# The MLP's matmuls of a hybrid decoder layer walk their 256 columns in interleaved chunks

## The chip, the cores and the metric

The program runs on 1 core of one Trainium2 chip. The metric is the device time of one execution in microseconds (us). Everything is computed in float32; the large products use the float32r type for both operands.

## What is computed

One decoder layer over 256 tokens with 16 learned meta tokens ahead of them and a width of 2048. Three token mixers (HGRN2, Mamba-2, RWKV-7) share a normed input and one combined projection, are gated, merged and projected. Only the channel mixer behind them is touched by the change:

```python
u = rmsnorm(h, ln2_w[l])
h = h + valid * (jnp.square(jax.nn.relu(u @ w_mlp_in[l])) @ w_mlp_out[l])
...
return rmsnorm(h, lnf_w)[:, CHUNK:]
```

`w_mlp_in` is 2048 x 8192 and `w_mlp_out` 8192 x 2048.

## The kernel before

Activations are held transposed: channels on the 128 partitions, tokens along the free dimension. A tile `[128, 16, 256]` is 2048 channels of 256 tokens. Each float32 operand is split into a high and a low part of type float32r, and a product is the sum of three: high by high, low by high weights, high by low weights.

`weights` (L213) fetches a weight piece of 128 x 1024 floats through SyncE's queue (L222, tile `raw`), copies it on ScalarE to the high part `wh` (L201) and takes the difference on VectorE for the low part `wl` (L202). Three buffers stand for each of `wh` and `wl`; weights are fetched and split ahead of the products that use them.

`product` (L229) makes one output tile of 128 channels by 256 tokens in a PSUM buffer `pt` (three of them in turn). For the MLP it issues 16 x 3 = 48 matmuls (L237, L238, L239). Each loads a 128 x 128 piece of weights into TensorE and streams 256 columns, the tokens, of one slice of the activations past it; all 48 accumulate on the same 256 places of PSUM.

The MLP (L1179 to L1204) runs over four quarters of the hidden width, `qd` 0 to 3. Each quarter has two stages of 16 products, so 768 matmuls to a stage, and there are eight stages in this order, called stage 1 to 8 below:

- stages 1, 3, 5, 7 (`mi`): the activations `zh`, `zl` by `w_mlp_in`; ScalarE takes the ReLU out of PSUM (L1185), VectorE squares (L1187), and the result is split into `hh`, `hl`.
- stages 2, 4, 6, 8 (`mo`): `hh`, `hl` by `w_mlp_out`; in stage 2 ScalarE copies the sum to `macc` (L1192), in stages 4 and 6 VectorE adds it there (L1194), and in stage 8 VectorE multiplies it by the norm's factor `r2` (L1200) and adds it to the residual `h1` (L1201).

The last norm follows: squares are summed over channels by a matmul with ones (L1206, L1209), and 12 tiles on VectorE and 4 on GpSimd are scaled (L1214) and stored (L1216).

Instructions are put in order by a scheduler at build time. On TensorE the products of the MLP follow each other in program order, stage after stage.

Of the kernel before, what the change touches and what calls it, by code (L numbers as in the profile page):

```python
# [20 lines left out]
KT = D // P  # L21
# [129 lines left out]
def tile_hybrid(ctx: ExitStack, tc: tile.TileContext, a, out, dbg=None):  # L151
    nc = tc.nc
    dbg = dbg or {}
    mult, add, sub = ALU.mult, ALU.add, ALU.subtract
    act, vec, pe = nc.scalar, nc.vector, nc.tensor

    def pool(stack, name, side=None, space=None, bufs=1):
        kw = {"side": side} if side else {}
        if space:
            kw["space"] = space  # L160
        return stack.enter_context(tc.tile_pool(name=name, bufs=bufs, reuse_waits="tile", **kw))
# [13 lines left out]
    def V(k, j=0, n=1, rows=slice(0, P)):  # L175
        return vecs[rows, VCOL[k] + j:VCOL[k] + j + n]
# [13 lines left out]
    def uname(s):  # L190
        cnt[0] += 1
        return f"{s}_{cnt[0]}"

    def trunk_psum(w):
        return ps_t.tile([P, 512], F32, tag="t", bufs=3, name=uname("pt"))[:, :w]
# [4 lines left out]
    def split(dst_h, dst_l, src):  # L200
        act.copy(dst_h, src)  # L201
        vec.tensor_tensor(dst_l, src, dst_h.bitcast(F32), sub)  # L202
# [10 lines left out]
    def weights(key, ahead=True):  # L213

        first, n = PIECE[key]
        parts = []
        for k in range(n):
            with tc.high_priority() if ahead else ExitStack():
                n_raw[0] += 1
                rpool, bufs = more_raw[n_raw[0] % len(more_raw)]  # L220
                raw = rpool.tile([P, 8, P], F32, tag="raw", bufs=bufs, name=uname("raw"))
                nc.sync.dma_start(raw, a["w"][first + k])  # L222
                wh = wp.tile([P, 8, P], F32R, tag="wh", bufs=3, name=uname("wh"))
                wl = wp.tile([P, 8, P], F32R, tag="wl", bufs=3, name=uname("wl"))
                split(wh, wl, raw)
            parts.append((wh, wl))
        return parts

    def product(key, hi, lo, tok, kts=KT, ahead=True):  # L229

        n = tok.stop - tok.start
        ps = trunk_psum(n)
        last = kts // 8 - 1
        for k, (wh, wl) in enumerate(weights(key, ahead)):
            for j in range(8):
                kt = 8 * k + j
                pe.matmul(ps, lhsT=wh[:, j], rhs=hi[:, kt, tok], start=(kt == 0), stop=False)  # L237
                pe.matmul(ps, lhsT=wh[:, j], rhs=lo[:, kt, tok], start=False, stop=False)  # L238
                pe.matmul(ps, lhsT=wl[:, j], rhs=hi[:, kt, tok], start=False,  # L239
                          stop=(k == last and j == 7))  # L240
        return ps

# [56 lines left out]
    def proj(key, tok=ALL, ahead=True):  # L299
        ps = product(key, uh, ul, tok, ahead=ahead)  # L300
        vec.tensor_tensor(ps, ps, rstd1[:, tok], mult)
        return ps
# [40 lines left out]
    for k in range(2):  # L343
        t = r1.tile([P, T + 1], F32, name=f"prev{k}")
# [19 lines left out]
    ps = proj("wl", ahead=False)  # L364
# [3 lines left out]
    ps = proj("aldt", ahead=False)  # L368
    shifted(ps, 25, alr[0:112], slice(0, 112))
    for j in range(2):  # L370
        ps = proj(("gl", j), REAL2)
# [155 lines left out]
    r2 = {}  # L527
# [552 lines left out]
    RT = slice(0, NR)  # L1080

    def branch_parts(o):
        hi = gp.tile([P, 8, NR], F32R, tag="oh", bufs=2, name=uname("oh"))
        lo = gp.tile([P, 8, NR], F32R, tag="ol", bufs=2, name=uname("ol"))
        for k in range(4):
            s = slice(2 * k, 2 * k + 2)
            split(hi[:, s], lo[:, s], o[:, s])
        return hi, lo
# [6 lines left out]
    def up_first(c, hi, lo):  # L1095
        g = gate_back("gr", c)
        ps = product(("upr", c), hi, lo, RT, 8)
        vec.tensor_tensor(mixed[:, c], ps, g, mult)

    def up_next(n, c, hi, lo, g):  # L1100
        ps = product((n, c), hi, lo, RT, 8)
        t = gp.tile([P, NR], F32, tag="bt", bufs=2, name=uname("bt"))
        vec.tensor_tensor(t, ps, g, mult)
        vec.tensor_tensor(mixed[:, c], mixed[:, c], t, add)
# [8 lines left out]
    hi, lo = branch_parts(o_r)  # L1113
# [4 lines left out]
    hi, lo = branch_parts(o_m)  # L1118
# [10 lines left out]
    hi, lo = branch_parts(o_h)  # L1129
# [14 lines left out]
    zh = ep.tile([P, 16, NR], F32R, name="zh")  # L1144
    zl = ep.tile([P, 16, NR], F32R, name="zl")
    acc2 = ep.tile([P, NR], F32, name="acc2")
    r2 = ep.tile([P, NR], F32, name="r2")
    macc = ep.tile([P, 16, NR], F32, name="macc")

    def et(tag, bufs=2):  # L1150
        return ep.tile([P, NR], F32, tag=tag, bufs=bufs, name=uname(tag))

    def add_square(c, src):
        s = et("sqe")
        act.activation(s, src, AF.Square)
        if c == 0:
            vec.tensor_copy(acc2, s)
        else:
            vec.tensor_tensor(acc2, acc2, s, add)

    for c in range(16):
        xr = et("xr", 3)
        nc.scalar.dma_start(xr, a["xt"][:, c, NM:])
        ps = product(("out", c), mh, ml, RT)
# [9 lines left out]

    act.activation(r2, pn, AF.Ln, bias=eps_n, scale=1.0 / D)
    act.activation(r2, r2, AF.Exp, scale=-1.0)
    st_y = ExitStack()
    yp = pool(st_y, "yp", side="right")
    for qd in range(4):  # L1179
        hh = yp.tile([P, 16, NR], F32R, tag="hh", bufs=2, name=uname("hh"))  # L1180
        hl = yp.tile([P, 16, NR], F32R, tag="hl", bufs=2, name=uname("hl"))
        for c in range(16):
            ps = product(("mi", 16 * qd + c), zh, zl, RT)
            r = et("rl")
            act.activation(r, ps, AF.Relu)  # L1185
            s = et("rs")
            vec.tensor_tensor(s, r, r, mult)  # L1187
            split(hh[:, c], hl[:, c], s)
        for c in range(16):
            ps = product(("mo", qd, c), hh, hl, RT)  # L1190
            if qd == 0:
                act.copy(macc[:, c], ps)  # L1192
            elif qd < 3:
                vec.tensor_tensor(macc[:, c], ps, macc[:, c], add)  # L1194
            if qd == 2:
                vec.tensor_tensor(macc[:, c], macc[:, c], r2, mult)
                vec.tensor_tensor(h1[:, c], h1[:, c], macc[:, c], add)
            if qd == 3:
                t = et("rs")
                vec.tensor_tensor(t, ps, r2, mult)  # L1200
                vec.tensor_tensor(h1[:, c], h1[:, c], t, add)  # L1201
                if c < 15:
                    add_square(c, h1[:, c])
                    act.activation(h1[:, c], h1[:, c], AF.Copy, scale=V("lnf", c))  # L1204
# [110 lines left out]
```

## Time and profile before

| What | us |
|---|---|
| median of 2 runs | 1935.1 (1934.91 to 1935.28) |
| the profiled execution's own time | 1936.93 |
| its span, first to last instruction | 1935.1 |
| TensorE busy with matmuls in it | 1906.0 (98%) |
| the eight MLP stages in it, one after the other | 733.6 (from 1187.18 to 1920.77) |

The span is what the profile's views cover; the execution's own time is 1.8 us more. PE is TensorE's matmuls, PEld its weight loads, DVE VectorE, ACT ScalarE, POOL GpSimd, SPq SyncE's queue. A matmul's duration in a row runs from its start to its modelled end and overlaps with those of the next ones; how fast TensorE works is told by how many matmuls it starts in a stretch.

### The profile page before, as it was taken

To read this page: it belongs to the slowest core of one execution; us is meant where nothing else is said; L and a number is where in the kernel's file an instruction comes from. 1 tells how busy PE (TensorE), PEld (TensorE's weight loads), DVE (VectorE), ACT (ScalarE), POOL (GpSimd) and SP (SyncE) were. 2 spreads that over 40 slices of the span, in tenths; PEclk is the share of its full clock that TensorE was granted. 3 is DMA by queue.
4 is the path that set the end of the run, shared out by engine and by line. 5 is a ranking of instruction groups with operands and counts; after the bars stand their busy time and mean duration, and the time that the engine had idled before them with its cause. 6 is when DMAs were issued, how large, how long until landed. Compare 5 with 4: busy or idle time off the path is not lost.

```text
span 1935.1 us, 39773 instructions
## 1 busy us (share of the span) xinstructions
PE 1906.0 (98%) x16220; PEld 1866.0 (96%) x16220; DVE 1242.9 (64%) x1992; ACT 1048.3 (54%) x1857; POOL 185.5 (10%) x318
## 2 busy tenths in 40 slices
PE   6999999999999999999999999999999999999997
PEld 6999999999999999999999999999999999999997
DVE  7878676567956566777677765544455555665565
ACT  5666666566556667766564455444444344334453
POOL 4020111111111111112111000000000000000000
PEclk9999999999999999999999999999999999999999
DMA  5556544445554445445656776555555555555552
GB/s 211 183 179 202 164 150 135 146 154 158 175 174 147 145 144 193 144 150 168 200 168 213 247 218 190 182 184 185 185 186 185 186 183 181 185 185 183 185 185 99
DMA packets 104119, 340.39 MB, mean 176 GB/s; under 512 B 18216, under 2 KB 21432, under 8 KB 103936
## 3 DMA queue, kind: packets, MB, share of 16 engines
q1 hardware_dynamic: 91904, 315.25, 51.0%
q0 software_dynamic: 8576, 17.67, 3.0%
q10 hardware_dynamic: 3456, 4.93, 0.7%
q8 instruction: 127, 2.08, 0.5%
q14 instruction: 56, 0.46, 0.1%
HBM read 327.72 MB, written 10.08 MB: 175 GB/s over the span
## 4 chain that ended last, share of the span: by engine, by line
PE 97%; DVE 1%; DMA 0%; issue 0%; ACT 0%; SPq 0%; DVEq 0%; POOLq 0%
PE pt L239 29%; PE pt L237 29%; PE pt L238 29%; PE px L1025 1%; PE px L551 1%; PE px L657 0%; PE px L639 0%; PE px L694 0%; PE px L565 0%; PE px L559 0%; DVE macc L1214 0%; PE px L480 0%; PE px L623 0%; PE px L627 0%; PE px L661 0%; PE px L848 0%
## 5 line engine op out<-in xcount | busy, mean ns | idle before, releaser
L202 DVE TENSOR_TENSOR wl<-raw,wh 128x1024 fp32r<-128x1024 f32 x592 | 725.6, 1226 | 452.1 <-ACT wh L201 444.8
L201 ACT CAST wh<-raw 128x1024 fp32r<-128x1024 f32 x592 | 620.4, 1049 | 706.2 <-PE pt L238 491.1
L237 PE MATMUL pt<-uh,wh 128*128 128x256 f32 (+3 forms) x2048 | 587.6, 287 | 9.2 <-ACT wh L201 9.2
L239 PE MATMUL pt<-uh,wl 128*128 128x256 f32 (+3 forms) x2048 | 587.9, 287 | 4.0 <-DVE wl L202 4.0
L238 PE MATMUL pt<-ul,wh 128*128 128x256 f32 (+3 forms) x2048 | 587.6, 287 | 1.7 <-DVE ul L285 1.7
L237 PEld LDWEIGHTS pt<-uh,wh 128*128 128x128 f32 x2048 | 387.8, 189 | 12.6 <-ACT wh L201 9.2
L239 PEld LDWEIGHTS pt<-uh,wl 128*128 128x128 f32 x2048 | 387.7, 189 | 8.1 <-DVE wl L202 4.6
L238 PEld LDWEIGHTS pt<-ul,wh 128*128 128x128 f32 x2048 | 387.2, 189 | 6.3 <-DVE ul L285 2.6
L239 PE MATMUL pt<-zh,wl 128*128 128x256 f32 x1024 | 290.0, 283 | 0.0
L238 PE MATMUL pt<-zl,wh 128*128 128x256 f32 x1024 | 289.8, 283 | 0.0
L237 PE MATMUL pt<-zh,wh 128*128 128x256 f32 x1024 | 289.8, 283 | 0.0
L239 PE MATMUL pt<-hh,wl 128*128 128x256 f32 x1024 | 288.0, 281 | 0.0
L238 PE MATMUL pt<-hl,wh 128*128 128x256 f32 x1024 | 288.0, 281 | 0.0
L237 PE MATMUL pt<-hh,wh 128*128 128x256 f32 x1024 | 287.8, 281 | 0.0
L237 PEld LDWEIGHTS pt<-zh,wh 128*128 128x128 f32 x1024 | 196.6, 192 | 0.0
L239 PEld LDWEIGHTS pt<-zh,wl 128*128 128x128 f32 x1024 | 196.6, 192 | 0.0
L238 PEld LDWEIGHTS pt<-zl,wh 128*128 128x128 f32 x1024 | 196.6, 192 | 0.0
L237 PEld LDWEIGHTS pt<-hh,wh 128*128 128x128 f32 x1024 | 192.8, 188 | 0.0
L238 PEld LDWEIGHTS pt<-hl,wh 128*128 128x128 f32 x1024 | 192.7, 188 | 0.0
L239 PEld LDWEIGHTS pt<-hh,wl 128*128 128x128 f32 x1024 | 192.7, 188 | 0.0
L239 PE MATMUL pt<-oh,wl 128*128 128x256 f32 x384 | 108.3, 282 | 0.0
L237 PE MATMUL pt<-oh,wh 128*128 128x256 f32 x384 | 108.2, 282 | 0.0
(451 smaller groups left out, 2388.0 us busy)
## 6 DMA issues: line engine op xcount, KB each, us to landing
raw<-in_w SPq DMA_DIRECT2D x592, 512.0 KB, 3.5
rcb<-sc_rc SPq DMA_DIRECT2D x8, 256.0 KB, 4.1
sc_gr<-gt POOLq DMA_DIRECT2D x16, 128.0 KB, 3.7
sc_gm<-gt POOLq DMA_DIRECT2D x16, 128.0 KB, 3.6
sc_gh<-gt POOLq DMA_DIRECT2D x16, 128.0 KB, 3.7
gin<-sc_gr POOLq DMA_DIRECT2D x16, 128.0 KB, 3.0
gin<-sc_gm POOLq DMA_DIRECT2D x16, 128.0 KB, 3.1
gin<-sc_gh POOLq DMA_DIRECT2D x16, 128.0 KB, 3.4
```

Source lines behind the costliest of these rows:

```text
L201: act.copy(dst_h, src)
L202: vec.tensor_tensor(dst_l, src, dst_h.bitcast(F32), sub)
L237: pe.matmul(ps, lhsT=wh[:, j], rhs=hi[:, kt, tok], start=(kt == 0), stop=False)
L238: pe.matmul(ps, lhsT=wh[:, j], rhs=lo[:, kt, tok], start=False, stop=False)
L239: pe.matmul(ps, lhsT=wl[:, j], rhs=hi[:, kt, tok], start=False, stop=(k == last and j == 7))
L551: pe.matmul(pk[e][:, c], lhsT=kt_[er, t], rhs=ar[er, :, t], start=True, stop=True)
L1025: pe.matmul(px[br, 2 * i + c], lhsT=xc, rhs=xc, start=True, stop=True)
```

## The change

`product` gets two views: `view` is laid over the moving operand (the 256 columns that are streamed) and, unless `view_out` is given, over the PSUM places that are written. `chunks(b, c)` cuts the 256 columns into `c` equal parts and takes `b` columns of the first part, `b` of the second and so on, then the next `b` of the first. Each column is still written to a place of its own and all 48 matmuls of a product use one order, so each sum has the same terms.

```diff
-    def product(key, hi, lo, tok, kts=KT, ahead=True):
+    def product(key, hi, lo, tok, kts=KT, ahead=True, view=lambda t: t, view_out=None):
...
+        po = (view_out or view)(ps)
...
-                pe.matmul(ps, lhsT=wh[:, j], rhs=hi[:, kt, tok], start=(kt == 0), stop=False)
+                pe.matmul(po, lhsT=wh[:, j], rhs=view(hi[:, kt, tok]), start=(kt == 0), stop=False)
...
+    def chunks(b, c=2):
+
+        return lambda t: t.rearrange("p (c a b) -> p a c b", c=c, b=b)
+
+    plain = lambda t: t
+
+    orders = [[chunks(16), chunks(16, 4)], [chunks(8), plain], [chunks(4), plain], [chunks(2), chunks(8)]]
...
-            ps = product(("mi", 16 * qd + c), zh, zl, RT)
+            ps = product(("mi", 16 * qd + c), zh, zl, RT, view=orders[qd][0])
...
-            ps = product(("mo", qd, c), hh, hl, RT)
+            if qd < 2:
+                ps = product(("mo", qd, c), hh, hl, RT, view=orders[qd][1])
+            elif qd == 2:
+
+                ps = product(("mo", qd, c), hh, hl, RT, view_out=chunks(8))
+                ps = chunks(8)(ps)
+            else:
+
+                ps = product(("mo", qd, c), hh, hl, RT, view=orders[qd][1], view_out=plain)
+                ps = ps.rearrange("p (a c b) -> p c a b", c=2, b=8)
             if qd == 0:
                 act.copy(macc[:, c], ps)
             elif qd < 3:
-                vec.tensor_tensor(macc[:, c], ps, macc[:, c], add)
+                m = macc[:, c] if qd == 1 else macc[:, c].rearrange("p (a c b) -> p a c b", c=2, b=8)
+                vec.tensor_tensor(m, ps, m, add)
...
                 t = et("rs")
-                vec.tensor_tensor(t, ps, r2, mult)
+                vec.tensor_tensor(t.rearrange("p (c a b) -> p c a b", c=2, b=8), ps,
+                                  r2.rearrange("p (c a b) -> p c a b", c=2, b=8), mult)
```

| Stage | columns read | places written |
|---|---|---|
| 1 | chunks of 16 from 2 halves | the same order |
| 2 | chunks of 16 from 4 quarters | the same order |
| 3 | chunks of 8 from 2 halves | the same order |
| 4 | in one run, as before | in one run, as before |
| 5 | chunks of 4 from 2 halves | the same order |
| 6 | in one run | chunks of 8; VectorE reads them back in runs of 8 |
| 7 | chunks of 2 from 2 halves | the same order |
| 8 | chunks of 8 from 2 halves | in one run; VectorE reads them back in runs of 8 |

No instruction changes its place on any engine. On TensorE, where stage 1 ends and stage 2 begins, this stands before (the shape at the end of a row is that of the places written; `pt` is the PSUM buffer, `zh`, `zl`, `hh`, `hl` the activations, `wh`, `wl` the weights):

```order
L237 MATMUL pt_16165<-zh,wh_16174 128x256
L238 MATMUL pt_16165<-zl,wh_16174 128x256
L239 MATMUL pt_16165<-zh,wl_16175 128x256
L237 MATMUL pt_16232<-hh_15158,wh_16235 128x256
L238 MATMUL pt_16232<-hl_15159,wh_16235 128x256
L239 MATMUL pt_16232<-hh_15158,wl_16236 128x256
```

At the same place on TensorE the changed kernel has:

```order
L239 MATMUL pt_16165<-zh,wh_16174 128x8x2x16
L240 MATMUL pt_16165<-zl,wh_16174 128x8x2x16
L241 MATMUL pt_16165<-zh,wl_16175 128x8x2x16
L239 MATMUL pt_16232<-hh_15158,wh_16235 128x4x4x16
L240 MATMUL pt_16232<-hl_15159,wh_16235 128x4x4x16
L241 MATMUL pt_16232<-hh_15158,wl_16236 128x4x4x16
```

The same buffers follow each other; only the shape differs: 8 x 2 chunks of 16, then 4 x 4 chunks of 16. The second place on TensorE is the end of stage 6 and the start of stage 7, before:

```order
L237 MATMUL pt_21324<-hh_19290,wh_21333 128x256
L238 MATMUL pt_21324<-hl_19291,wh_21333 128x256
L239 MATMUL pt_21324<-hh_19290,wl_21334 128x256
L237 MATMUL pt_21390<-zh,wh_21393 128x256
L238 MATMUL pt_21390<-zl,wh_21393 128x256
L239 MATMUL pt_21390<-zh,wl_21394 128x256
```

And in the changed kernel:

```order
L239 MATMUL pt_21324<-hh_19290,wh_21333 128x16x2x8
L240 MATMUL pt_21324<-hl_19291,wh_21333 128x16x2x8
L241 MATMUL pt_21324<-hh_19290,wl_21334 128x16x2x8
L239 MATMUL pt_21390<-zh,wh_21393 128x64x2x2
L240 MATMUL pt_21390<-zl,wh_21393 128x64x2x2
L241 MATMUL pt_21390<-zh,wl_21394 128x64x2x2
```

Again nothing moved: stage 6 writes 32 runs of 8 places, and stage 7 writes (and reads) 128 runs of 2. That stage 8 reads in runs of 8 is not seen in such rows, since it writes in one run.

## Rows read from the trace of the kernel before

**Rows 1.** The page: busy time of the engines, and the chain that ended last.

```profile
PE 1906.0 (98%) x16220; PEld 1866.0 (96%) x16220; DVE 1242.9 (64%) x1992; ACT 1048.3 (54%) x1857; POOL 185.5 (10%) x318
...
PE 97%; DVE 1%; DMA 0%; issue 0%; ACT 0%; SPq 0%; DVEq 0%; POOLq 0%
```

**Rows 2.** Windows of the eight MLP stages in turn, all instructions.

```profile
core 0: us, PE busy (x) PEld busy (x) DVE busy (x) ACT busy (x) POOL busy (x), PEclk, DMA share, GB/s
1187.18:1279.75 92.57, 92.57 (x772) 92.52 (x771) 50.38 (x65) 44.08 (x67) 0.00 (x0) 1.00 0.57 182
1279.75:1370.88 91.13, 91.13 (x770) 91.13 (x769) 39.87 (x34) 38.12 (x49) 0.00 (x0) 1.00 0.58 185
1370.88:1463.04 92.16, 92.16 (x770) 92.16 (x769) 49.28 (x62) 42.66 (x63) 0.00 (x0) 1.00 0.57 183
1463.04:1554.18 91.14, 91.14 (x770) 91.14 (x769) 46.07 (x49) 34.11 (x34) 0.00 (x0) 1.00 0.59 185
1554.18:1646.33 92.15, 92.15 (x770) 92.15 (x769) 49.72 (x63) 42.40 (x62) 0.00 (x0) 1.00 0.57 183
1646.33:1737.47 91.14, 91.14 (x770) 91.14 (x769) 57.48 (x79) 34.10 (x34) 0.00 (x0) 1.00 0.57 186
1737.47:1829.63 92.16, 92.16 (x770) 92.16 (x769) 50.48 (x65) 42.40 (x62) 0.00 (x0) 1.00 0.58 183
1829.63:1920.77 91.14, 91.14 (x770) 91.14 (x769) 54.90 (x77) 45.56 (x62) 0.00 (x0) 1.00 0.46 145
```

**Rows 3.** Waits in the MLP, longest first: who waited, total us, times, longest.

```profile
DVE wl L202 <- ACT wh L201: 292.1, 220, 3.9
ACT wh L201 <- PE pt L238: 203.7, 126, 1.8
...
DVE macc L1194 <- PE pt L239: 24.3, 30, 2.9
```

**Rows 4.** Single lines of TensorE: ns min/median/max, first and last start, form.

```profile
L495 PE MATMUL px<-ar,tkb x16: 191/248/270, 80.0 to 474.8; 128*96 128x32 f32 x16
L613 PE MATMUL px<-xtb,gt x128: 196/196/217, 225.7 to 683.4; 128*32 128x32 f32 x128
L551 PE MATMUL px<-ar,kt x64: 376/376/480, 213.7 to 628.8; 64*128 64x256 f32 x64
L1064 PE MATMUL px<-am,itm x16: 377/378/381, 806.4 to 1026.4; 96*128 96x256 f32 x16
```

**Rows 5.** Single lines of VectorE and ScalarE that read or write in short runs.

```profile
L1015 ACT ACTIVATE x<-sfx x64: 292/309/334, 722.0 to 1011.6; 128x128 f32<-128x128 f32 x64
L520 DVE COPY bigA<-bigB x2: 1052/1077/1102, 213.5 to 540.1; 68x1024 f32<-68x1024 f32 x2
```

**Rows 6.** Single lines that take the MLP's sums out of PSUM.

```profile
L1194 DVE TENSOR_TENSOR macc<-pt,macc x32: 418/425/426, 1471.6 to 1737.7; 128x256 f32<-128x256 f32 x32
L1200 DVE TENSOR_TENSOR rs<-pt,r x16: 418/424/426, 1838.1 to 1921.0; 128x256 f32<-128x256 f32 x16
```

**Rows 7.** Timeline of the end: start, us, what, and idle time before it.

```profile
1920.66 0.28 PE L239 MATMUL pt<-hh,wl 128*128 128x256 f32 x1
...
1920.98 0.42 DVE L1200 TENSOR_TENSOR rs<-pt,r 128x256 f32<-128x256 f32 x1 [3.90 <-PE pt L239]
1921.44 0.43 DVE L1201 TENSOR_TENSOR h<-h,rs 128x256 f32<-128x256 f32 x1
1921.90 0.42 ACT L1208 ACTIVATE sqe<-h 128x256 f32<-128x256 f32 x1 [4.74 <-DVE h L1201]
```

More of the change, by code (lines that the diff above doesn't have):

```diff
@@ L236, in product @@
                 kt = 8 * k + j
-                pe.matmul(ps, lhsT=wh[:, j], rhs=hi[:, kt, tok], start=(kt == 0), stop=False)
-                pe.matmul(ps, lhsT=wh[:, j], rhs=lo[:, kt, tok], start=False, stop=False)
-                pe.matmul(ps, lhsT=wl[:, j], rhs=hi[:, kt, tok], start=False,
+                pe.matmul(po, lhsT=wh[:, j], rhs=view(hi[:, kt, tok]), start=(kt == 0), stop=False)
+                pe.matmul(po, lhsT=wh[:, j], rhs=view(lo[:, kt, tok]), start=False, stop=False)
+                pe.matmul(po, lhsT=wl[:, j], rhs=view(hi[:, kt, tok]), start=False,
                           stop=(k == last and j == 7))
```

## The prediction

> **What bounds the kernel now.** I read the page first, then the windows of the MLP, then its waits, then single lines that resemble what the change makes. The page says that matmuls are in flight for 1906.0 of 1935.1 us and that 97% of the chain that ended last is TensorE [rows 1]. That alone proves little, since a matmul's row overlaps its neighbours, so the reader should look at counts: in each of the eight stages TensorE is busy without a gap, at a granted clock of 1.00, that is 2.4 GHz [rows 2]. A stage holds 768 matmuls by the code (the row counts one or two more, those that straddle the edges). Stages 3, 5 and 7 take 92.16 us, 120.0 ns a matmul; stages 2, 4, 6 and 8 take 91.14 us, 118.7 ns; stage 1, at 92.57 us, has a few tenths of start in it. 256 columns at one a cycle of 2.4 GHz would be 106.7 ns, so each matmul has 12 to 13 ns on top, and the columns cannot be going at half that pace.
>
> Who waits is told by the third view: in the MLP VectorE and ScalarE wait for one another and for TensorE (292.1 and 203.7 us), and no row has TensorE waiting for anybody [rows 3]. VectorE is busy 40 to 57 of some 91 us in a stage and ScalarE 34 to 46 [rows 2]. So one ns more or less per matmul is felt in full at the end, and work of other engines is not.
>
> **The change part by part.** No instruction is added, removed or moved, no transfer changes its place and no wait is added; what differs is the order of addresses within one instruction.
>
> Matmuls. 7 of 8 stages change, 7 x 768 = 5376 matmuls. In six stages (all but 4 and 6) the streamed columns come in runs, in six (all but 4 and 8) the PSUM places are written in runs: 16 runs a matmul in stages 1 and 2, 32 in stage 3, 64 in stage 5, 32 in stage 6 (writing only), 128 in stage 7, 32 in stage 8 (reading only). The columns stay 256. The question is whether a break between runs costs anything. The trace of before has no matmul with short runs on the writing side, and few on the reading side, so I bound it by the nearest rows.
>
> - Reading, TensorE: L495 streams 32 columns as two runs of 16, and its shortest row is 191 ns; L613 streams 32 columns in one run at 196 ns. L551 streams 256 columns as two runs of 128 at 376 ns, L1064 256 columns in one run at 377 to 378 ns [rows 4]. These lines differ in partitions too, and their ends are modelled, but neither pair shows a price for a break.
> - Many breaks, another engine: L1015 on ScalarE reads and writes 128 elements of which the first round of its loop has 128 runs of one and the last one run of 128. All 64 instructions lie between 292 and 334 ns [rows 5]. If the whole spread were due to runs, a break would cost 42 / 127 = 0.33 ns.
> - Supply of separate places: L520 on VectorE reads 1024 elements, each 128 bytes from the one before, in 1077 ns, 1.05 ns each [rows 5]. Stage 7 asks for a new place every second column, 0.83 ns at 2.4 GHz, a little faster than that row shows the memory to serve; stage 5 asks for one in 1.67 ns, and the others ask less often.
> - Below nothing: the trace has two paces for the same plain matmul, 120.0 and 118.7 ns, that go with the tile that is read. If the new order moved all 5376 to the quicker one, 5376 x 1.3 ns = 7 us would go.
>
> So the ends for the matmuls are -7 us and, at 0.33 ns for each of 16 + 16 + 32 + 64 + 32 + 128 + 32 = 320 runs in 768 matmuls, +81 us; doubling of stage 7 alone would be +92 us. I take 0, because the two rows that are TensorE's own show none, and they are nearest.
>
> The Trainium skill speaks against this choice: "PSUM — Partial Sum Buffer", section Specifications (TRN2), says that any access pattern that is not contiguous slows matmuls significantly. By that sentence the six stages that write in runs would suffer even at runs of 16, which no row here shows; it is the third rival below. The skill's "Advanced Engine Details and Errata", section Memory Cachelines, is milder: two consecutive elements should stand together in PSUM, and two hits on a line of SBUF are enough. By that sentence all eight orders are free, and its sum would be mine.
>
> Element-wise work. Stage 6's adds (L1194, 16 of the 32) and stage 8's products (L1200, 16) read PSUM in runs of 8. They take 425 and 424 ns [rows 6]. At worst I give each the double, 16 x 0.42 = 6.8 us to a stage; VectorE has over 33 us free in each of these stages and the three PSUM buffers give it two products, 11 us, to catch up, so this is hidden. Only the last L1200 stands on the path: it follows the last matmul and the sum of squares waits for it [rows 7]. Between 0 and 0.4 us; I take 0, by the same spread in rows of ScalarE.
>
> Sum. 1936.9 us for the profiled execution, plus 0. It is 1.8 us above the runs' median, so against the median this is 1935.1; with a few tenths for the tail and for the breaks I say 1935.5.
>
> **The rivals.**
> Stage 7 starves. With runs of two columns, TensorE wants a new place each 0.83 ns. If the memory gives one in 1.05 ns, as L520's row has it, 128 places take 134.6 ns in place of 106.7, a growth of 15 to 28 ns a matmul depending on whether the 12 to 13 ns on top remain: 768 x 15 to 28 = 11 to 21 us, 1946 to 1957. If a run of two costs as much as a run of four, the stage doubles: 1935 + 92 = 2027. For it: it is the only stage that asks for more than any row has shown. Against it: L520 may be at the pace of VectorE, not of the memory. It decides once a place takes longer than 0.83 ns.
>
> Every break costs a fixed bubble. At 0.33 ns, 81 us: 2016. For it: the spread of L1015. Against it: L551 and L495, which have a break and no price. It passes 2% (39 us, about what a measurement of this kernel tells from no change) from 39000 / (320 x 768) = 0.16 ns a break.
>
> Writing in runs costs TensorE the double, whatever the run's length. Stages 1, 2, 3, 5, 6 and 7 together are 551 us [rows 2], so 1935 + 551 = 2486. For it: no row of before has such a write, so nothing excludes it. Against it: nothing in the trace but analogy.
>
> Faster. To win 39 us, 5376 matmuls would have to lose 7.2 ns each of the 12 to 13 on top of their columns. The rows show 1.3 ns between tiles, nothing like it.
>
> **How the numbers follow.** No change within 10 us: 0.62. Stage 7 slower by 11 to 21 us: 0.10, within 2% too. Stage 7 doubled: 0.08. A bubble for each break above 0.16 ns: 0.09. Writes doubled: 0.08. Faster by over 2%: 0.03. So within 2% is 0.72, slower 0.25, faster 0.03. The likeliest case's own range is 1928 to 1945: 7 us for the quicker pace below, 10 above. To leave out no more than 2 in 10 the range goes up to the doubled stage 7 and the bubble: 1928 to 2030; what is left out is the doubled writes, the gain and the worst of the bubbles.
>
> **What would show it.** In the windows of the changed kernel each stage should take 91.1 to 92.6 us, with 768 matmuls and the same idle rows. Stage 4 is plain and must stay at 91.1 in any case; if it moves, the cause is not the order. Stage 7 alone long means supply; growth by 16, 16, 32, 64, 32, 128, 32 means a price per break; stages 1, 2, 3, 5, 6, 7 long alike, with 8 as before, means writes; stage 8 long with 6 as before means reads. TensorE appearing among those who wait in the MLP would show that I misjudged the cover on VectorE.

## The result and the profile after

The changed kernel takes 1988.1 us (two runs, 1988.06 to 1988.18) against 1935.1 before. The ratio is 1.0274, 95% interval 1.0249 to 1.0298: slower, by 53 us. That is inside the range, but well above the time that I gave as likeliest (1935.5); how my cases stand to it is told further below.

The page of the profile after, the same two lines as in [rows 1]:

```profile
PE 1958.9 (99%) x16220; PEld 1919.4 (97%) x16220; DVE 1243.0 (63%) x1992; ACT 1052.4 (53%) x1857; POOL 186.5 (9%) x318
...
PE 97%; DVE 1%; DMA 0%; issue 0%; ACT 0%; SPq 0%; DVEq 0%; POOLq 0%
```

As many matmuls as before, 53 us more of TensorE, nothing of note elsewhere. Where it went is seen in the windows of the eight stages, with the columns of [rows 2]:

```profile
1185.00:1277.59 92.59, 92.59 (x772) 92.53 (x771) 50.38 (x65) 44.08 (x67) 0.00 (x0) 1.00 0.55 183
1277.59:1369.76 92.17, 92.17 (x771) 92.17 (x770) 39.89 (x34) 38.13 (x49) 0.00 (x0) 1.00 0.56 183
1369.76:1464.48 94.72, 94.72 (x771) 94.72 (x769) 49.30 (x62) 42.94 (x63) 0.00 (x0) 1.00 0.54 178
1464.48:1555.62 91.14, 91.14 (x771) 91.14 (x769) 46.09 (x49) 34.11 (x34) 0.00 (x0) 1.00 0.56 185
1555.62:1654.59 98.97, 98.97 (x770) 98.97 (x769) 49.72 (x63) 44.08 (x62) 0.00 (x0) 1.00 0.50 171
1654.59:1746.75 92.16, 92.16 (x770) 92.16 (x769) 57.51 (x79) 34.16 (x34) 0.00 (x0) 1.00 0.55 183
1746.75:1877.30 130.55, 130.55 (x770) 130.55 (x769) 50.47 (x65) 43.18 (x62) 0.00 (x0) 1.00 0.39 130
1877.30:1972.02 94.72, 94.72 (x770) 94.72 (x769) 54.92 (x77) 45.62 (x62) 0.00 (x0) 1.00 0.42 138
```

Each window runs from the first matmul of a stage to the first of the next, so its length over 768 is the pace. Against [rows 2]: stage 1 as before; stage 2 +1.0 us; 3 +2.6; 4, the plain one, as before to the hundredth; 5 +6.8; 6 +1.0; 7 +38.4 (170.0 ns a matmul in place of 120.0); 8 +3.6. Together 53.4 us. The granted clock is 1.00 in all of them, so nothing of this is the clock. What is left of the difference lies ahead of the MLP, which starts at 1185.0 in place of 1187.2 here and between 1184.8 and 1187.5 in the runs below (but for the last, which changes what stands ahead of it).

The waits in the MLP after, and the two lines that now read PSUM in runs of 8:

```profile
DVE wl L202 <- ACT wh L201: 343.2, 221, 4.0
...
ACT wh L201 <- PE pt L240: 212.5, 126, 3.0
```

```profile
L1213 DVE TENSOR_TENSOR macc<-pt,macc x32: 418/425/426, 1473.0 to 1747.0; 128x256 f32<-128x256 f32 x32
...
L1219 DVE TENSOR_TENSOR rs<-pt,r x16: 418/425/425, 1886.1 to 1972.2; 128x256 f32<-128x256 f32 x16
```

As in [rows 3], no row has TensorE waiting for anybody in the MLP; the others wait a little longer for it. The two lines take what they took in [rows 6]. So the time is inside the matmuls.

### The profile page after: what moved, and what is told of

Read it like the earlier page. It is cut to its first block, busy times and chain, and to the rows that moved or that the text cites. A ratio compares the mean times of both kernels' runs of the same rounds, so it can differ in the third digit from the quotient of the medians.

```text
span 1986.4 us, 39772 instructions
## 1 busy us (share of the span) xinstructions
PE 1958.9 (99%) x16220; PEld 1919.4 (97%) x16220; DVE 1243.0 (63%) x1992; ACT 1052.4 (53%) x1857; POOL 186.5 (9%) x318
## 4 chain that ended last, share of the span: by engine, by line
PE 97%; DVE 1%; DMA 0%; issue 0%; ACT 0%; SPq 0%; DVEq 0%; POOLq 0%
PE pt L240 30%; PE pt L239 30%; PE pt L241 29%; PE px L1027 1%; PE px L553 1%; PE px L659 0%; PE px L641 0%; PE px L696 0%; PE px L567 0%; PE px L561 0%; DVE macc L1234 0%; PE px L482 0%; PE px L625 0%; PE px L629 0%; PE px L663 0%; PE px L850 0%
## 5 line engine op out<-in xcount | busy, mean ns | idle before, releaser
L240 PE MATMUL pt<-zl,wh 128*128 128x256 f32 x1024 | 308.8, 302 | 0.0
L239 PE MATMUL pt<-zh,wh 128*128 128x256 f32 x1024 | 307.7, 300 | 0.0
L241 PE MATMUL pt<-zh,wl 128*128 128x256 f32 x1024 | 307.3, 300 | 0.0
```

Source lines behind the costliest of these rows:

```text
L239: pe.matmul(po, lhsT=wh[:, j], rhs=view(hi[:, kt, tok]), start=(kt == 0), stop=False)
L240: pe.matmul(po, lhsT=wh[:, j], rhs=view(lo[:, kt, tok]), start=False, stop=False)
L241: pe.matmul(po, lhsT=wl[:, j], rhs=view(hi[:, kt, tok]), start=False, stop=(k == last and j == 7))
```

## The experiments

All stages take 768 matmuls and can be read one by one, so one kernel tests up to eight orders. In the kernels below a list gives to each stage the order of reading and of writing: `(b, c)` is `chunks(b, c)`, so `(1, 2)` takes single columns from the two halves in turn, and `N` (None) is one run. In two of the tests `("d", k)` takes single columns in turn from two places that are `k` columns apart (0, k, 1, k + 1, ...), and `("s", k)` takes every `k`-th column, from the two halves in turn. What is written in another order than it is read is put right where ScalarE or VectorE takes it out of PSUM.

### Reading apart from writing

```diff
+    stages = [((2, 2), N), (N, (2, 2)), ((4, 2), N), (N, (4, 2)),
+              (N, (2, 2)), ((2, 2), N), (N, N), ((4, 2), N)]
...
-            ps = product(("mi", 16 * qd + c), zh, zl, RT, view=orders[qd][0])
+            ps = product(("mi", 16 * qd + c), zh, zl, RT, view=order_of(rd), view_out=order_of(wr))
```

> Splits reading from writing; every product stays as it is. Stages 1 and 6 read in runs of 2 and write in one run; stages 3 and 8 read in runs of 4 and write in one run; stages 2 and 5 read in one run and write in runs of 2; stage 4 writes in runs of 4; stage 7 is plain. Theory 'reading' (TensorE is held up by fetching the columns): stages 1 and 6 take about 170 ns a matmul (130 us), 3 and 8 about 129 ns (99 us), and 2, 4, 5 and 7 stay at 118.7 to 121 ns (91 to 93 us). Theory 'writing' (PSUM takes short runs slowly): 2 and 5 at 170 ns, 4 at 129 ns, and 1, 3, 6, 8 at 119 to 121 ns. If both sides share the price, each of 1, 2, 5, 6 lies between, near 145 ns.

Measured: the windows of the first six stages of this kernel.

```profile
1184.85:1313.27 128.42, 128.42 (x773) 128.37 (x771) 50.39 (x65) 44.16 (x67) 0.00 (x0) 1.00 0.39 133
1313.27:1404.41 91.14, 91.14 (x770) 91.14 (x769) 39.88 (x34) 38.11 (x49) 0.00 (x0) 1.00 0.54 184
1404.41:1501.71 97.30, 97.30 (x770) 97.30 (x769) 49.28 (x62) 43.17 (x63) 0.00 (x0) 1.00 0.51 174
1501.71:1592.86 91.15, 91.15 (x771) 91.15 (x770) 46.07 (x49) 34.09 (x34) 0.00 (x0) 1.00 0.55 185
1592.86:1685.01 92.15, 92.15 (x771) 92.15 (x769) 49.71 (x63) 42.43 (x62) 0.00 (x0) 1.00 0.54 183
1685.01:1812.99 127.98, 127.98 (x770) 127.98 (x769) 57.57 (x79) 33.96 (x34) 0.00 (x0) 1.00 0.39 133
```

The two stages that read in runs of 2 take 167 ns a matmul, the two that write in runs of 2 take 118.7 and 120.0, the plain paces. Stages 3 and 8, which read in runs of 4, take 126.7 and 129.5 ns. The price is for reading. That it is 167 ns here and was 170 in the changed kernel, which also wrote in runs of 2, was not explained.

### Writing alone

```diff
+    stages = [(N, (16, 2)), (N, (16, 4)), (N, (4, 2)), (N, (2, 64)),
+              (N, (2, 4)), (N, (4, 32)), (N, (8, 2)), (N, N)]
```

> Only the writing order differs from before, one order to a stage; reads are in one run. Stages 1 to 7 write in runs of 16 from two halves, 16 from four quarters, 4 from two halves, 2 in steps of 16 bytes, 2 from four quarters, 4 in steps of 32 bytes, 8 from two halves; stage 8 is plain. Theory 'reading': all within 118.7 to 121 ns a matmul (91 to 93 us a stage). Theory 'writing': 4 and 5 about 170 ns (130 us), 3 and 6 about 129 ns (99 us), 7 about 123 ns, 1 and 2 about 120 ns.

Measured: 1935.0 us in a single run, against 1935.5 for before on the same chip. Two of its windows, the stages that write in runs of 2:

```profile
1461.10:1552.24 91.14, 91.14 (x771) 91.14 (x769) 46.08 (x49) 34.10 (x34) 0.00 (x0) 1.00 0.56 185
1552.24:1644.39 92.15, 92.15 (x770) 92.15 (x769) 49.71 (x63) 42.41 (x62) 0.00 (x0) 1.00 0.55 183
```

All eight stages stand at the lengths of [rows 2] within 0.02 us. Seven orders of writing, down to runs of 2, cost nothing. The sentence of the Trainium skill that any pattern in PSUM that is not contiguous slows matmuls ("PSUM — Partial Sum Buffer", Specifications (TRN2)) does not hold in any of them. Single columns were not tried on the writing side.

### The changed kernel without stage 7's order

```diff
-    orders = [..., [chunks(2), chunks(8)]]
+    stages = [..., (N, N), ((8, 2), N)]
```

> The changed kernel with stage 7 alone put back to the plain order. If the stages' prices add up (stage 7 took 130.4 us in place of 92.0), 1988.1 - 38.4 = 1949.7 us, which is 0.8% above before. If stage 7's length has another cause than its order, it stays at 130 us and the time near 1988.

Measured: 1949.2 us, ratio to before 1.0074 (1.0057 to 1.0090). The windows of its stages 5 to 7:

```profile
1557.22:1654.49 97.27, 97.27 (x770) 97.27 (x769) 49.70 (x63) 42.94 (x62) 0.00 (x0) 1.00 0.50 174
1654.49:1745.64 91.15, 91.15 (x771) 91.15 (x769) 57.48 (x79) 34.11 (x34) 0.00 (x0) 1.00 0.54 185
1745.64:1837.79 92.15, 92.15 (x770) 92.15 (x769) 50.47 (x65) 42.40 (x62) 0.00 (x0) 1.00 0.55 183
```

Stage 7 is 39 of the 53 us, and the stages add up. Stage 6 is back at 91.15 with its writes still in runs of 8, so the +1.0 us there is not the order's; stage 5 with the same order took 98.97 us in one program and 97.27 in the other. What decides these one or two us I have not found.

### Which orders of reading are slow

Eight orders of reading were set against three theories of what makes one slow. A stretch of 16 bytes is four columns, the first of them at a multiple of 16 bytes.

```diff
+    stages = [((2, 64), N), ((2, 4), N), ((1, 128), N), ((1, 64), N),
+              ((1, 2), N), ((4, 32), N), ((2, 16), N), ((16, 2), N)]
```

> Only the reading order differs from before, one order to a stage; writes are in one run. Stage 1: runs of 2, each 16 bytes behind the last (64 of them, twice). Stage 2: runs of 2 from four quarters. Stage 3: every second column, then the others. Stage 4: every fourth column, four times. Stage 5: single columns from two halves in turn. Stage 6: runs of 4, each 32 bytes behind the last. Stage 7: runs of 2, each 64 bytes behind the last. Stage 8: runs of 16 from two halves. Theory 'places of 16 bytes' (what counts is how often a new stretch of 16 bytes is asked for, 1.33 ns each from stage 7 of the changed kernel): 128 visits and 170 ns in stages 1, 2, 3 and 7, 256 visits and about 340 ns in 4 and 5, about 129 ns in 6, 119 to 120 in 8. Theory 'runs' (what counts is how many breaks the columns have): 170 ns in 1, 2 and 7, about 340 ns in 3, 4 and 5. Theory 'distance' (the jump between two halves, 512 bytes, is what costs): 1, 6 and 7 near 120 ns, 2 and 5 long.

Measured: all eight windows.

```profile
1185.49:1360.14 174.65, 174.65 (x772) 159.83 (x771) 50.37 (x65) 44.10 (x67) 0.00 (x0) 1.00 0.29 100
1360.14:1534.26 174.12, 174.12 (x770) 158.99 (x768) 39.88 (x34) 38.22 (x49) 0.00 (x0) 1.00 0.28 97
1534.26:1708.35 174.09, 174.09 (x770) 159.46 (x768) 49.31 (x62) 42.60 (x63) 0.00 (x0) 1.00 0.28 97
1708.35:1887.54 179.19, 179.19 (x769) 160.51 (x768) 46.19 (x49) 33.95 (x35) 0.00 (x0) 1.00 0.28 94
1887.54:1973.33 85.79, 85.79 (x770) 85.78 (x768) 49.63 (x63) 42.31 (x62) 0.00 (x0) 1.00 0.55 190
1973.33:2065.47 92.14, 92.14 (x770) 92.14 (x769) 57.58 (x80) 34.04 (x34) 0.00 (x0) 1.00 0.56 184
2065.47:2232.72 167.25, 167.25 (x770) 157.69 (x769) 50.49 (x65) 42.34 (x62) 0.00 (x0) 1.00 0.30 104
2232.72:2324.90 92.18, 92.18 (x769) 92.17 (x768) 54.92 (x77) 45.53 (x62) 0.00 (x0) 1.00 0.41 138
```

All three theories fall. Runs of 2 in steps of 16 bytes (stage 1, 227 ns) are worse than runs of 2 from two halves (167), so distance is not it. Every fourth column (stage 4, 256 visits to a stretch) takes 233 ns and every second (stage 3, 128 visits) 227, so it is not so much for each visit. Stage 1, with 128 breaks, takes as long as stage 3, with 256, so it is not so much for each break. And stage 5, single columns from two halves in turn, with as many breaks as any, takes 111.7 ns: quicker than the plain order by 8.3 ns.

Two theories are weighed in what follows. "Line kept", which I went on with from here: one sequence of columns, in which two stretches of 16 bytes are held open, and a price for each opening. "Two streams", which I set up only after the results of the next two tests and which is tested in the third: the 1st, 3rd, 5th column and the 2nd, 4th, 6th are fetched apart, and each of the two sequences wants successive columns from one stretch of 16 bytes. In the plain order each stream finds two, with single columns from two halves four, in runs of 2 from two halves one at a time.

### Distance between the two places

```diff
+    stages = [(("d", 64), N), (("d", 32), N), (("d", 16), N), (("d", 8), N),
+              (("d", 4), N), (("d", 2), N), ((1, 2), N), ((1, 2), N)]
...
+            return lambda t: t.rearrange("p (d c a) -> p d a c", c=2, a=s[1])
```

> Single columns from two places in turn, the distance alone differs: 64, 32, 16, 8, 4 and 2 columns in stages 1 to 6 (256, 128, 64, 32, 16 and 8 bytes), 128 columns (512 bytes) in 7 and 8. Theory 'two places at once': short (112 ns) down to some distance and about 227 ns from there on. Theory 'line kept': near 112 ns for every distance, since only two stretches of 16 bytes are open at a time. Stages 7 and 8 at 111.7 ns whichever tile is read; if the quick pace belongs to the tile of stage 7 alone, stage 8 stays at 118.7 ns.

Measured: the windows of stages 5 (4 columns apart, 16 bytes), 6 (2 columns, 8 bytes) and 8.

```profile
1530.61:1616.37 85.76, 85.76 (x770) 85.76 (x769) 49.59 (x63) 42.32 (x62) 0.00 (x0) 1.00 0.63 196
1616.37:1707.52 91.15, 91.15 (x771) 91.15 (x769) 57.56 (x80) 34.14 (x34) 0.00 (x0) 1.00 0.59 186
...
1793.28:1879.04 85.76, 85.76 (x771) 85.76 (x770) 54.96 (x78) 45.48 (x62) 0.00 (x0) 1.00 0.49 155
```

From 512 bytes down to 16 it is 111.7 ns, and at 8 bytes it is the plain pace, 118.7. "Two places at once" falls, since no distance comes anywhere near 227 ns. "Line kept" did not foresee the step at 8 bytes: there the columns 0, 2, 1, 3 lie in one stretch. "Two streams", set up afterwards, fits it: one stream gets 0, 1, then 4, 5, which is two to a stretch, as in the plain order; at 16 bytes (0, 4, 1, 5, 2, 6, 3, 7) it gets 0, 1, 2, 3.

### An offset of 8 bytes, and more than two places

```diff
-    zh = ep.tile([P, 16, NR], F32R, name="zh")
+    zh = ep.tile([P, 16, NR + 4], F32R, name="zh")[:, :, 2:NR + 2]
...
+    stages = [(N, N), ((1, 4), N), ((16, 2), N), ((4, 4), N),
+              ((8, 2), N), ((1, 8), N), ((4, 2), N), ((1, 16), N)]
```

> The tiles that stages 1, 3, 5 and 7 read begin 8 bytes off a multiple of 16: stage 1 plain, 3 runs of 16, 5 runs of 8, 7 runs of 4, each from two halves. Theory '16 bytes at a time': a run of 4 now lies over two stretches of 16 bytes, so stage 7 rises from 127 ns to between 167 ns (as runs of 2 from two halves) and 227 ns, stage 5 to between 130 and 170 ns, and stage 1 stays at 120 ns. Theory 'runs': 120, 120, 123 and 127 ns, as without the offset. Stages 2, 6 and 8 read single columns from 4, 8 and 16 places in turn, stage 4 runs of 4 from four quarters. Theory 'two places at once' (two columns are fetched together when they come from parts far from each other): 2, 6 and 8 rise towards 220 ns as neighbours in the sequence come to lie in the same half; theory 'line kept' (a fetched stretch of 16 bytes is kept for a few visits): 2 near 112 ns and 6 or 8 above 220 ns; 4 near 127 ns by both.

Measured: the windows of stages 1 to 7.

```profile
1187.46:1280.44 92.98, 92.98 (x773) 92.92 (x771) 50.37 (x65) 44.02 (x67) 0.00 (x0) 1.00 0.57 182
1280.44:1387.95 107.51, 107.51 (x770) 107.51 (x769) 39.86 (x34) 38.08 (x49) 0.00 (x0) 1.00 0.49 157
1387.95:1502.48 114.53, 114.53 (x770) 114.53 (x769) 49.27 (x62) 42.62 (x63) 0.00 (x0) 1.00 0.45 148
1502.48:1606.37 103.89, 103.89 (x770) 103.89 (x769) 46.23 (x49) 35.22 (x34) 0.00 (x0) 1.00 0.50 162
1606.37:1741.05 134.68, 134.68 (x771) 134.68 (x769) 49.69 (x63) 42.36 (x62) 0.00 (x0) 1.00 0.40 127
1741.05:1912.56 171.51, 171.51 (x769) 158.97 (x769) 57.32 (x79) 34.20 (x35) 0.00 (x0) 1.00 0.31 101
1912.56:2041.96 129.40, 129.40 (x770) 129.40 (x769) 50.41 (x65) 42.31 (x62) 0.00 (x0) 1.00 0.39 127
```

The plain order keeps its pace (121 ns), but runs of 16, 8 and 4 that begin 8 bytes off a multiple of 16 take 149, 175 and 168 ns, where runs of the same lengths without the offset took 120, 123 and 127 to 129. So runs count by how they lie in stretches of 16 bytes, and "runs" falls; "16 bytes at a time" is right on stages 1 and 7 and had stage 5 too low (at most 170). Single columns from 4, 8 and 16 places take 140, 223 and 220 ns, as "two places at once" had it, which the test of distance excludes; "line kept" had 112 for the first. Stage 4, runs of 4 from four quarters, takes 135 ns, where both had near 127: a miss that I can't account for. 140 lies between the paces: by "two streams" alone, with each stream between two places, it should be near 227. That would fit if a stretch is not lost at once when a stream leaves it, which was not tested. The 167 ns of the runs of 2 from two halves and the 168 of the offset runs of 4 fall in the same gap.

### Two streams, forecast on new orders

```diff
+        if s and s[0] == "s":
+            return lambda t: t.rearrange("p (c e k) -> p k e c", c=2, k=s[1])
...
+    stages = [((1, 2), N), (("s", 2), N), (("d", 4), N), (("s", 4), N),
+              (("s", 2), N), ((2, 2), N), (("d", 8), N), (("d", 4), N)]
```

> Reads alone differ; zh and zl begin 8 bytes off a multiple of 16, hh and hl do not. Theory 'two streams': of the sequence of columns the 1st, 3rd, 5th and the 2nd, 4th, 6th are fetched apart, and each of the two sequences must find two successive columns in one stretch of 16 bytes to keep pace (four are a little better, one is half pace). Theory 'line kept': one sequence, with two stretches of 16 bytes kept open, and the price is for each opening. Stage 1 (offset, single columns from two halves): 112 ns by both. Stage 2 (columns 0, 128, 2, 130, 4, ..., then the odd ones): two streams 118.7 to 120 ns; line kept between 167 and 227 ns, since every stretch is opened twice. Stage 3 (offset, 0, 4, 1, 5, 2, 6, 3, 7): two streams 118 to 121 ns. Stage 4 (0, 128, 4, 132, 8, ..., four rounds): 227 to 233 ns by both. Stage 5 (as 2, with the offset): two streams 118 to 122 ns; line kept over 167 ns. Stage 6 (runs of 2 from two halves, as stage 7 of the changed kernel): 167 ns. Stage 7 (offset, 0, 8, 1, 9, ...): 112 to 120 ns. Stage 8 (0, 4, 1, 5, ... without offset): 112 ns.

Measured: the windows of stages 2 to 6.

```profile
1271.75:1362.89 91.14, 91.14 (x771) 91.14 (x769) 39.97 (x35) 38.12 (x49) 0.00 (x0) 1.00 0.59 186
1362.89:1452.57 89.68, 89.68 (x771) 89.68 (x769) 49.29 (x62) 42.69 (x63) 0.00 (x0) 1.00 0.60 188
1452.57:1628.34 175.77, 175.77 (x771) 159.48 (x769) 46.17 (x49) 33.97 (x35) 0.00 (x0) 1.00 0.30 99
1628.34:1722.86 94.52, 94.52 (x769) 94.52 (x768) 49.70 (x63) 42.38 (x62) 0.00 (x0) 1.00 0.54 173
1722.86:1854.27 131.41, 131.41 (x771) 131.41 (x770) 57.57 (x79) 34.39 (x34) 0.00 (x0) 1.00 0.41 130
```

Stage 2 is the one that tells the theories apart: 0, 128, 2, 130, 4, ... has a jump at each column and opens every stretch twice, and it takes 91.14 us, 118.7 ns, the same as the plain order on the same tile. "Line kept" wanted over 167 ns. Stage 4, with one column of a stretch to each stream, takes 229 ns. Stages 3 and 5 came 1 ns outside their bounds on either side (116.8 and 123.1), stages 7 and 8 inside (113.8 and 111.7), and stage 6 took 171 ns where I had written 167. Counting by streams gives an estimate for the offset runs too, made after the fact: in runs of 16 each stream visits 5 stretches where the plain order has 4, so 106.7 x 5/4 and 12 to 13 on top, 145 to 146 ns (measured 149); in runs of 8 it visits 6 in place of 4, 172 to 173 ns (measured 175). What two streams does not work out are 135 ns for runs of 4 from four quarters and 123 to 129 for runs of 8 and 4 from two halves, where it has the plain pace, and 140 and 167 to 171, where it has 227. Among the latter is stage 7 of the changed kernel.

### Half of the weights

```diff
-                pe.matmul(po, lhsT=wh[:, j], rhs=view(lo[:, kt, tok]), start=False, stop=False)
+                pe.matmul(po[:mw], lhsT=wh[:, j, :mw], rhs=view(lo[:, kt, tok]), start=False, stop=False)
...
+    stages = [((1, 2), N), ((1, 2), N), (N, N), (N, N), (N, N), ((2, 64), N), ((2, 2), N), ((1, 2), N)]
```

> Stages 3, 4, 7 and 8 load only 64 of the 128 columns of weights in 46 of the 48 matmuls of each product, so half of the output channels lack most of their sum there. Reads: stages 1, 2 and 8 single columns from two halves in turn, 3, 4 and 5 plain, 6 runs of 2 in steps of 16 bytes, 7 runs of 2 from two halves. Theory 'shared reading' (the weight load and the columns compete for the same reads): the plain stages 3 and 4 fall from 120 and 118.7 ns to 112 ns or less, and stage 7 from 167 ns to about 155 ns or less. Theory 'columns alone': 3 and 4 stay at 120 and 118.7 ns, 7 at 167 ns; 1, 2 and 8 take 111.7 ns each.

Measured: stages 3, 4, 7 and 8, the ones with half of the weights.

```profile
1357.28:1444.80 87.52, 87.52 (x770) 87.52 (x769) 49.22 (x62) 42.63 (x63) 0.00 (x0) 1.00 0.60 193
1444.80:1534.45 89.65, 89.65 (x770) 89.65 (x769) 46.10 (x50) 34.05 (x34) 0.00 (x0) 1.00 0.59 189
...
1802.37:1930.37 128.00, 128.00 (x769) 110.42 (x768) 50.39 (x65) 42.30 (x62) 0.00 (x0) 1.00 0.39 129
1930.37:2014.31 83.94, 83.94 (x771) 83.94 (x770) 54.79 (x77) 45.30 (x62) 0.00 (x0) 1.00 0.50 156
```

Neither theory: the plain paces fall from 120.0 and 118.7 to 114.0 and 116.7 ns, not to 112, and the runs of 2 stay at 166.7. Stage 8, the quick order, falls from 111.7 to 109.3. So a part of the 12 to 13 ns above one column a cycle goes with the weight load or with the places written, of which half are gone as well (the test does not part the two). The price of the slow order stays within what runs of 2 from two halves vary by between programs (166.6 to 171.1 ns).

### An order quicker than the plain one, in all stages

```diff
+    stages = [((1, 2), N)] * 8
```

> All eight stages read single columns from two halves in turn and write in one run. If the pace of the fifth stage of the reading test (111.7 ns) holds in all: 8 x 768 x 111.7 ns = 686 us in place of 733.6, so 1935.1 - 47.7 = 1887 us, 2.5% under before. If the pace is bound to what stands around that one stage, between 1887 and 1935 us. If reading sums out of PSUM in single columns held up ScalarE or VectorE so far that TensorE waits, above 1935 us.

Measured: 1889.0 us, ratio to before 0.9756 (0.9739 to 0.9772). The windows of stages 2 and 3, alike for both tiles:

```profile
1273.36:1359.12 85.76, 85.76 (x771) 85.76 (x770) 39.94 (x35) 38.09 (x49) 0.00 (x0) 1.00 0.61 197
1359.12:1444.88 85.76, 85.76 (x771) 85.76 (x770) 49.18 (x62) 42.58 (x63) 0.00 (x0) 1.00 0.62 197
```

The eight stages take 686.5 us in place of 733.6, and reading the sums back in single columns holds nobody up. With the same order in the four projections ahead of the MLP (the edit of the output projection is shown, the three of the branches are changed alike):

```diff
-        ps = product(("out", c), mh, ml, RT)
-        vec.tensor_tensor(h1[:, c], ps, xr, add)
+        ps = product(("out", c), mh, ml, RT, view=by_halves, view_out=lambda t: t)
+        vec.tensor_tensor(halves_out(h1[:, c]), halves_ps(ps), halves_out(xr), add)
```

> Single columns from two halves in turn in all eight MLP stages, and also in the three branch projections (1152 matmuls at about 117.7 ns in before) and the output projection (768 at 118.7 ns). If 111.7 ns holds there: 1889.0 - 1152 x 6.0 ns - 768 x 7.0 ns = 1889.0 - 6.9 - 5.4 = 1876.7 us, 3.1% under before. If the projections of the branches, which stand between the chains of the last mixer, wait for other work, less of the 6.9 us comes back and the time lies between 1877 and 1884 us.

Measured: 1876.6 us, ratio to before 0.9693 (0.9677 to 0.9709), as worked out; the division of the gain between the four projections was not measured by itself. This version beats both kernels, by 3.1% and 5.6% (1876.6 / 1988.1).

## Why the prediction was right or wrong

- **What bounds.** Right. TensorE had no slack in the MLP: in the result and in the first nine runs, what the eight stages gained or lost together came out at the end within 1.4 us, and the tenth came out as summed.
- **The cost of a break, taken as 0.** This is the step that failed: in its place the windows show +53.4 us, 38.4 of them in stage 7. I took 0 because L495 and L551 were "nearest", and they are rows of runs of 16 and 128 columns. For runs of 16 they spoke nearly true (stage 1 unchanged, 1.0 us more in stage 2); about runs of 2 they say nothing, and I let them stand for all lengths. I had myself noted that stage 7 asks for more than any row shows, and then took the value of the rows that ask for less. I also read them wrongly. Of L495 I took the shortest row, 191 ns; its median is 248, against 196 for L613 [rows 4]. And 376 against 377 ns compares modelled ends, where the pace is told by starts. By the code these lines multiply plain float32. On the timeline of before, eight L551 take 1.07 us from the first's start to the next line's, 134 ns each, and two L1064 take 0.43 us, 215 ns each, where the MLP's matmuls take 119 to 120. The two lines, of 64 and 96 partitions, differ far more in pace than in modelled duration, so the pair tells nothing of a break's price:

```profile
213.72 1.14 PE L551 MATMUL px<-ar,kt 64*128 64x256 f32 x8
214.79 0.39 PE L238 MATMUL pt<-ul,wh 128*128 128x256 f32 x1
...
806.40 0.59 PE L1064 MATMUL px<-am,itm 96*128 96x256 f32 x2
806.83 0.38 PE L1065 MATMUL px<-at,it 128*128 128x128 f32 x2
```

- **The time and the range.** Neither my likeliest case, no change within 10 us, nor a time within 2%, to which I gave 0.72, came true. The range covers 1988.1, but by luck: its upper part was there for stage 7 doubled (2027) and for a bubble of 0.16 to 0.33 ns at every break (1974 to 2016), and neither is what happened. Stage 7 came out between my two prices for it, and smaller costs in other stages came on top.
- **Stage 7 starves.** The rival with the right place, the reading side and the largest share: +38.4 us. I had priced it at 11 to 21 us by L520 or 92 by doubling. Its measure, a price for each new place, is wrong too: 256 visits to a stretch of 16 bytes cost little more than 128 in the reading test (233 and 227 ns). By "two streams", what counts is how many successive columns each of two streams finds within 16 bytes; that says why stage 7 is slow, but has it at 227 ns and not at the 170 measured, so its size stays open. What the Trainium skill says of SBUF in "Advanced Engine Details and Errata", Memory Cachelines, that two hits on a line are enough, agrees only if each of the two streams is counted: the plain order, with two each, keeps its pace (118.7 ns), one each is half pace (227 to 233). I had counted the hits over the whole sequence, by which stage 7 has its two, and so read the page as saying that it is free; counted like that, runs of 2 in steps of 16 bytes have their two as well, and took 227 ns.
- **Every break costs a bubble.** Not as put, for the price is not fixed. It is nothing in stage 1, 2.6 us / (768 x 32) = 0.10 ns in stage 3, 0.14 in stage 5, 0.15 in stage 8 and 0.39 in stage 7, above my bound of 0.33; and single columns from two halves, with 256 breaks, are quicker than none. Stages other than 7 do cost something, 13.7 us together when 7 is plain (1949.2 - 1935.5), and what runs of 8 and 4 pay for was not found.
- **Writes in runs.** Rightly held unlikely, and shown to be free down to runs of 2. The section of the Trainium skill that I called milder, Memory Cachelines in "Advanced Engine Details and Errata", also has the sentence that patterns in PSUM that are not contiguous slow matmuls significantly, so it did not side with me as plainly as I wrote; in none of the seven orders did that sentence hold.
- **Element-wise work.** Right: L1213 and L1219 are unchanged, and TensorE waits for neither.
- **Faster.** I wrote that the rows show 1.3 ns between tiles and nothing like 7.2 ns. That was true of the rows, and no bound: single columns from two places give 7.0 and 8.3 ns.

## What to carry to other kernels

Where matmuls bound a kernel, the order in which a float32r operand's columns are read is a cost of its own, and neither the waits nor the chain that ended last shows it; the count of matmuls per window does. Here runs of 16 begun on a multiple of 16 bytes cost at most 1.4 ns of some 119, runs of 8 cost 3 to 5 and runs of 4 between 1 and 17, so check the pace of any short run. Other orders of writing cost nothing here, down to pairs. And a bound taken from rows that ask for less than the change does is no bound: mark the stage that goes beyond every row and price it by itself.

## What was not expected of the hardware

Columns taken singly from two places at least 16 bytes apart stream at 111.7 ns for 256, where one run takes 118.7 to 120.0; at 2.4 GHz one a cycle would be 106.7. No distance from 16 to 512 bytes made a difference, as long as the tile began on a multiple of 16 bytes. That the fetch goes in two streams is a reading of some thirty orders, one of which it forecast against its rival; what in the chip does it was not seen. Open are the paces of 135, 140 and 167 to 171 ns, stage 7's own among them, and why one order took 126.7 ns in one program and 128.9 in another.
